# Moving a copy, a residual and a factor among ScalarE's and VectorE's work in a hybrid attention and pooling layer

## The chip, the core and the metric

The kernel runs on one core of a Trainium2 chip. The time is that of the device in microseconds (us) for one execution; the kernel before has a median of 1194.55 us over 3 runs (1194.26 to 1194.8). Lower is better. Two kernels computing the same output are compared: nothing in the arithmetic differs between them.

## The reference

One encoder layer over 4096 tokens of width 1024, in float32:

```
h    = RMSNorm(x) * pre_norm_g
q, k, v, g_a, u_p, g_p = split(h @ w_in)                  # w_in is 1024 x 2304
a    = banded_attention(q, k, v, bias, sink) * silu(g_a)  # 8 query heads, 2 kv heads, |i-j| <= 128
p    = pooling(u_p) * silu(g_p)                           # windows 2/4/8/16, a linear map per group
mix  = concat(a, p) @ w_out                               # 1024 x 1024
out  = x + RMSNorm(mix) * post_norm_g
```

In the attention each block of 128 queries sees three blocks of keys; a learned bias is added to the logits, and a learned sink takes part in the softmax.

## The kernel before

**Numbers and tiles.** A float32 operand is carried as two float16 tiles, a high part and the rest, so one product is three matmuls. `nc.tensor` is TensorE (PE in the profile), `nc.vector` VectorE (DVE), `nc.scalar` ScalarE (ACT), `nc.gpsimd` GpSimd (POOL), and `nc.sync` issues the DMAs (SP).

**Two stages.** The first, until about 480 us, normalises x, projects the gates and the pooling input, and writes parts of this to DRAM. The second goes backwards over 16 units of 256 tokens, from unit 15 to unit 0; a unit is two blocks of 128 queries, 2u and 2u+1. For a unit it projects k, v and q, forms the softmax of each block in two halves of four heads ("a visit"), and then multiplies the gated values with the output weights. The change touches only this last multiplication and what follows it.

**The output product.** It is a seven-product scheme over quarters of the matrices (`"11"`, `"22"`, `"12"`, `"s1"` to `"s4"`); the products are accumulated in three PSUM banks, `acc0` to `acc2`, and combined in float32 tiles `mo` on the way out. Product 11 goes into bank 0. `begin` (line 1568) lets ScalarE copy it to the upper half of `mo_0`, because it is wanted alone; product 12 is then accumulated on top of it in the same bank, so the first matmul of product 12 waits for the copy. When 12 is finished, two engines read bank 0: `square` (line 1573) on ScalarE sums squares for the norm, and `gain11` (line 1578) on VectorE multiplies by `post_norm_g` into the lower half of `mo_0`. The framework puts readers of one PSUM bank on different engines in the order in which the program names them, and makes the second wait for the first.

**The softmax of a visit.** Per head: `logits` on VectorE (line 1295) from PSUM, `exps` on ScalarE (1306), then once `denominators` on VectorE (1313 and the reciprocal 1316), then `probs` on ScalarE (1328, the scaled high part) and `rests` on VectorE (1336, the remainder), and last `turn` (1345), a transposing DMA from `pn` to `pt`, which `values` (1417, PE) reads.

**The end of a block.** `mean` computes the root on VectorE and GpSimd (1602, 1607), `residual` (1611) on VectorE forms `xr = mo * rs + xr` over 1024 columns, and `store` (1617) sends it out. `i = 0` is the unit's second block; its residual reads `mo_0`. There is one buffer for `mo_0` (`bufs=1`), so a unit's `begin` and the unit before it share that memory. GpSimd meanwhile runs `sum4` (1494), `low` (1456, the rest of a split) and a small copy of the sink's logit into the tiles `p` (1289), which the exponentials read.

**What sets the order.** Every call is put into a list with a due time, `due(t, fn, ...)`; `pe(us, ...)` advances the clock `now[0]` of the TensorE work by an estimate. The list is sorted by time and emitted in that order with manual scheduling: each engine executes its own instructions in exactly this order, and waits in that order. A due time matters only through the order of rows on an engine. The last units, 1 and 0, have a written table of their own, in which `gain11` already stands ahead of `square` and nothing is changed.

Of the kernel before, what the change touches and what calls it, by code (L numbers as in the profile page):

```python
# [19 lines left out]
D = 1024  # L20
# [19 lines left out]
O11, O12, O21, O22, OT1, OT2, OT4, OT3 = range(8)  # L40
# [94 lines left out]
def hybrid_layer(ctx: ExitStack, tc, io, out):  # L135
# [74 lines left out]
    with ExitStack() as actx:  # L210
# [689 lines left out]
        for j in range(4):  # L900
            ld(9.5 + 0.1 * j, wut[:, j], io["w_uT"][j], 0.5, w=[f"wut{j}"])
            z = turn("sq")
            for half in range(2):
                t = U0 + 4 * j + 2 * half
# [338 lines left out]
    def due(t, fn, *args):  # L1243
        plan.append((t, len(plan), fn, args))
# [261 lines left out]
    LO, HI = slice(0, 512), slice(512, D)  # L1506
# [123 lines left out]
    def pe(us, fn, *args):  # L1630

        due(now[0], fn, *args)
        now[0] += us
        return now[0]
# [27 lines left out]
    M = 2.6  # L1662

    def mix_p1(u):
        due(pe(M, product, u, "11", O11, 0) - 0.2, begin, u)

    def mix_p4(u):
        pe(M, product, u, "22", OT4, 2)

    def mix_p2(u):  # L1670
        t = pe(M, product, u, "12", O21, 0, True)
        due(t, square, u, 0, 0, 0)
        due(t + 0.1, gain11, u)

    def mix_p6(u):
        due(pe(M, product, u, "s2", OT2, 1), add, u, (0, HI), (0, HI), 1)
# [8 lines left out]
    def mix_p5(u):  # L1685
        t = pe(M, product, u, "s1", OT1, 1)
        due(t, add, u, (1, HI), (1, HI), 1)
        due(t + 0.7, square, u, 1, 1)
        due(t + 1.4, gain, u, 1, HI)
        finish(u, 1, t + 4.0)  # L1690

    def mix_p3(u):
        t = pe(M, product, u, "s4", O22, 1, True)
        due(t, add, u, (0, HI), (0, HI), 1)
        due(t + 0.7, square, u, 0, 1)
        due(t + 1.4, gain, u, 0, HI)
        finish(u, 0, t + 4.0, 6.4)

    def finish(u, i, t, late=0.0):

        due(t, mean, u, i)
        due(t + 2.0 + late, residual, u, i, slice(0, D))
        due(t + 3.4 + late, store, u, i, slice(0, D))

    u = NU - 1
# [10 lines left out]
    for b in reversed(range(2, NB)):  # L1718
        u = b // 2
# [13 lines left out]
        elif b == NB - 3:  # L1733
            due(free[1], load_wo, OT3)
            mix_p4(u + 1)
            mix_p1(u + 1)
            attend(b + 1)
            visit(b, 1)
            due(free[1], load_wo, OT1)
            due(free[1] + 8.0, load_wo, O22)  # L1740
            do_kv(u - 1, 1)
            mix_p2(u + 1)
            mix_p6(u + 1)
        elif b % 2:
            mix_p3(u + 2)
            do_kv(u - 1)
            attend(b + 1)
            visit(b, 1)
            mix_p4(u + 1)
            mix_p1(u + 1)  # L1750
            mix_p6(u + 1)
            mix_p2(u + 1)
        else:
            do_q(u - 1, 0, 2.0 * (b == NB - 2), int(b < NB - 4))
            if b < NB - 2:
                attend(b + 1)
            visit(b, 1)
            do_q(u - 1, 1, 2.0 * (b == NB - 2))
            due(now[0] + 2.1, load_x, u - 3)
            if b == NB - 2:  # L1760
                attend(b + 1)
            elif b > 2:
                mix_p7(u + 1)
                mix_p5(u + 1)
# [212 lines left out]
```

## Time and profile before

| what | value |
|---|---|
| median of 3 runs | 1194.55 us |
| the profiled execution | 1192.77 us |
| its span in the profile | 1190.9 us |
| granted TensorE clock | 0.999 |
| busy: PE, DVE, ACT, POOL | 1156.3, 939.4, 702.2, 302.5 us |
| second stage, 480 to 1190 us: PE, DVE, ACT | 691.8, 555.3, 435.7 us of 710 |

A timeline row gives start, duration, engine, line, operation, out<-in and count; in brackets stands the idle time before it and what ended it. Rows of one line that follow each other are merged: "x3" of 1.62 us is three instructions. Consecutive instructions of an engine overlap a little in the records. The profiled execution is a single one, 1.78 us below the median; its span leaves out 1.87 us of it.

### The profile page before, as it was taken

The numbers are of one execution on the slowest core, as the hardware profiler recorded it, in microseconds if no ns is written. First come the engines' busy times: TensorE is split into PE (matmuls) and PEld (weight loads), VectorE is DVE, ScalarE is ACT, GpSimd is POOL, SyncE is SP. The second block draws the span as 40 slices with busy tenths as digits, with TensorE's granted clock in tenths as the row PEclk, the third lists the DMA queues.
The fourth block names the chain that finished last, engine by engine and source line by source line (L and its number), as shares of the span: only waits on it lengthen the run. The fifth ranks groups of instructions, "written<-read, shape, count | busy, mean of one in ns | idle before, by whom it ended". The sixth has DMA issues, their size and how long they took to land. (4 is left out here: it accounts for less than half of the span.)

```text
span 1190.9 us, 31660 instructions
## 1 busy us (share of the span) xinstructions
PE 1156.3 (97%) x13176; PEld 887.1 (74%) x13176; DVE 939.4 (79%) x1834; ACT 702.2 (59%) x1459; POOL 302.5 (25%) x309
## 2 busy tenths in 40 slices
PE   5999999999999999899999999999999999999997
PEld 4998888888988888876667676676666767757643
DVE  6889996867888973567878877887887887788786
ACT  5865655545755541266566675666666666666672
POOL 0002111101101110202324433432532443343231
PEclk9999999999999999999999999999999999999999
DMA  8644587577657573387976875776876577587794
GB/s 313 213 122 153 167 274 249 171 239 257 222 169 248 160 208 118 115 253 198 234 180 135 202 194 121 197 194 162 173 187 173 139 203 180 137 189 159 157 248 124
DMA packets 292432, 224.51 MB, mean 189 GB/s; under 512 B 210704, under 2 KB 251920, under 8 KB 287680
## 3 DMA queue, kind: packets, MB, share of 16 engines
q1 hardware_dynamic: 292288, 222.48, 68.5%
q8 instruction: 103, 1.69, 0.6%
q14 instruction: 41, 0.34, 0.1%
HBM read 113.37 MB, written 60.33 MB: 146 GB/s over the span
## 5 line engine op out<-in xcount | busy, mean ns | idle before, releaser
L634 PEld LDWEIGHTS <-wq 128*128 128x128 f16 x4104 | 401.5, 98 | 52.7 <-issue 2.8
L634 PE MATMUL y<-xt,wq 128*128 128x256 f16 x1512 | 204.2, 273 | 0.9 <-ACT cc L742 0.9
L1336 DVE SCALAR_TENSOR_TENSOR pn<-p,rd,pn 128x384 f16<-128x384 f32 (+1 forms) x256 | 156.7, 654 | 30.5 <-ACT pn L1328 30.5
L1227 PE MATMUL aq<-xb,xb 128*128 128x256 f16 x1024 | 173.2, 273 | 0.0
L1306 ACT ACTIVATE p<-p,nm 128x385 f32<-128x385 f32 (+1 forms) x256 | 152.9, 599 | 33.3 <-DVE nm L1295 27.9
L1550 PE MATMUL ms<-wo,ys 128*128 128x512 f16 x720 | 162.9, 379 | 0.7 <-ACT pn L1328 0.6
L1295 DVE CUSTOM_DVE_ANT_0 p<-s,nt,nsink 128x384 f32<-128x384 f32 (+1 forms) x256 | 155.9, 666 | 1.3 <-PE s L1272 1.1
L1328 ACT ACTIVATE pn<-p,rd 128x384 f16<-128x384 f32 (+1 forms) x256 | 137.7, 598 | 30.1 <-issue 19.5
L1227 PEld LDWEIGHTS <-xb 128*128 128x128 f16 x1280 | 125.1, 98 | 22.8 <-issue 6.6
L1227 PE MATMUL aq<-xb,xt 128*128 128x256 f16 x512 | 139.6, 273 | 0.0
L1550 PEld LDWEIGHTS <-ys 128*128 128x128 f16 x720 | 69.0, 98 | 82.9 <-issue 3.0
L1550 PE MATMUL m<-wo,y 128*128 128x512 f16 x540 | 121.7, 379 | 6.0 <-ACT mo L1568 5.0
L304 POOL TENSOR_TENSOR yt<-yt,sg 128x512 f32<-128x512 f32 (+2 forms) x32 | 48.0, 1499 | 311.4 <-DVE yt L307 293.9
L1550 PEld LDWEIGHTS <-y 128*128 128x128 f16 x540 | 51.4, 98 | 71.7 <-issue 11.9
L1584 POOL TENSOR_TENSOR mo<-mo,gpost 128x512 f32<-128x512 f32 x39 | 63.8, 1635 | 96.3 <-ACT jkb L1573 95.1
L634 PE MATMUL plain<-xb,wq 128*128 128x256 f16 x576 | 68.8, 276 | 3.0 <-ACT xb L446 1.8
L1417 PE MATMUL o<-pt,vv 128*64 128x256 f16 x1128 | 68.0, 274 | 1.1 <-DMA pt<-pn 1.1
L634 PE MATMUL y<-xb,wq 128*128 128x256 f16 x504 | 68.8, 273 | 0.0
L634 PE MATMUL v<-xb,wq 128*128 128x256 f16 x504 | 68.6, 273 | 0.2 <-DVE cc L304 0.2
L1227 PEld LDWEIGHTS <-xt 128*128 128x128 f16 x640 | 62.6, 98 | 8.3
L634 PE MATMUL v<-xt,wq 128*128 128x256 f16 x504 | 68.6, 273 | 0.0
L634 PE MATMUL x<-xb,wq 128*128 128x256 f16 x504 | 68.3, 273 | 0.0
(207 smaller groups left out, 1852.8 us busy)
## 6 DMA issues: line engine op xcount, KB each, us to landing
nt<-in_xT SPq DMA_DIRECT2D x28, 512.0 KB, 5.3
x_scr<-xb SPq DMA_DIRECT2D x14, 1024.0 KB, 7.1
xb<-x_scr SPq DMA_DIRECT2D x14, 1024.0 KB, 7.5
xr<-in_x SPq DMA_DIRECT2D x28, 512.0 KB, 4.6
out<-xr SPq DMA_DIRECT2D x28, 512.0 KB, 2.6
xn<-in_x SPq DMA_DIRECT2D x27, 512.0 KB, 4.4
ga_scr<-cc SPq DMA_DIRECT2D x64, 128.0 KB, 2.1
raw<-in_w_out SPq DMA_DIRECT2D x16, 512.0 KB, 5.2
```

The source lines that it names most:

```text
L304: eng.tensor_tensor(out=out, in0=in0, in1=in1, op=op)
L634: nc.tensor.matmul(b[:, s], wq[:, slot[q, op], wv, s, k, :], x[:, xv, k, :], start=(first and k + s + wv + xv == 0), stop=(last and k == H ...
L1227: nc.tensor.matmul(acc, w[:, j, k, :], x[:, kh, v, kt, :], start=(n == 0), stop=(n == 3 * KT - 1),)
L1295: nc.vector.tensor_tensor_reduce(out=p_t[b, half][:, hh, :nk], in0=s_t[jj][:, gg, :nk], in1=bias[:, h, lo : lo + nk], scale=negc[:, h : h ...
L1306: nc.scalar.activation(p[:, hh, : nk + 1], p[:, hh, : nk + 1], AF.Exp, bias=nm_t[b, half][:, hh : hh + 1], scale=-1.0, accum_out=den_t[b, ...
L1328: nc.scalar.activation(prob_view(b, half)[:, 0, i], p_t[b, half][:, i, :nk], AF.Copy, scale=rd_t[b, half][:, i : i + 1],)
L1336: nc.vector.scalar_tensor_tensor(out=pn4[:, 1, i], in0=p_t[b, half][:, i, :nk], scalar=rd_t[b, half][:, i : i + 1], in1=pn4[:, 0, i], op0= ...
L1417: nc.tensor.matmul(o_ps[a, 2 * half : 2 * half + 2], v[:, vi, kt, a], pt[b, half][:, pi, g, :, i, :], start=(n == 0), stop=(n == last),)
L1550: nc.tensor.matmul(z_t[u, tag], y[:, k, yi, :], wo[o][:, wi, k, :], start=(n == 0 and acc is None), stop=(n == 3 * HK - 1), skip_group_che ...
L1584: eng.tensor_tensor(out=mo, in0=mo, in1=gpost[:, cs], op=ALU.mult)
```

## The change

Three edits in the functions that give due times:

- `mix_p1`: the copy of product 11 (`begin`) is due 0.8 us earlier.
- `mix_p2`: `gain11` is due first and `square` 0.1 us later; before, it was the other way round.
- `mix_p3`: the residual of the second block is issued as two halves of 512 columns, 0.7 us apart, where one of 1024 stood; `mean` and `store` keep their times. `finish` loses an argument that nobody uses any more.

```diff
     def mix_p1(u):
-        due(pe(M, product, u, "11", O11, 0) - 0.2, begin, u)
+        due(pe(M, product, u, "11", O11, 0) - 1.0, begin, u)
 ...
     def mix_p2(u):
         t = pe(M, product, u, "12", O21, 0, True)
-        due(t, square, u, 0, 0, 0)
-        due(t + 0.1, gain11, u)
+        due(t, gain11, u)
+        due(t + 0.1, square, u, 0, 0, 0)
 ...
         due(t + 1.4, gain, u, 0, HI)
-        finish(u, 0, t + 4.0, 6.4)
-
-    def finish(u, i, t, late=0.0):
+        due(t + 4.0, mean, u, 0)
+        due(t + 12.4, residual, u, 0, LO)
+        due(t + 13.1, residual, u, 0, HI)
+        due(t + 13.8, store, u, 0, slice(0, D))
+
+    def finish(u, i, t):
 
         due(t, mean, u, i)
-        due(t + 2.0 + late, residual, u, i, slice(0, D))
-        due(t + 3.4 + late, store, u, i, slice(0, D))
+        due(t + 2.0, residual, u, i, slice(0, D))
+        due(t + 3.4, store, u, i, slice(0, D))
```

ScalarE's rows around the copy in unit 9, before. `p_1` and `pn_1` are the exponentials and scaled probabilities of a visit, `m_9` is bank 0 with product 11 (and later 12), `jkb` the throwaway output of `square`, and the `ys` are operands of later products:

```order
L1306 ACTIVATE p_1_11431,den_1_11429<-p_1_11431,nm_1_11428 128x385 [waits DVE_49] x3
L1328 ACTIVATE pn_1_11460<-p_1_11431,rd_1_11430 128x384 [waits DMAHW4_49,DVE_49,Activation_49]
L1568 COPY mo_0_11463<-m_9_11443 128x512 [waits PE_49]
L1328 ACTIVATE pn_1_11460<-p_1_11431,rd_1_11430 128x384 [waits Activation_49]
L1328 ACTIVATE pn_1_11460<-p_1_11431,rd_1_11430 128x384
L1328 ACTIVATE pn_1_11460<-p_1_11431,rd_1_11430 128x384 [waits Activation_49]
L1452 CAST ys_9_11505<-at_11361 128x4x128
L1452 CAST ys_9_11507<-s_9_11411 128x4x128 [waits PE_49]
L1573 ACTIVATE jkb_00_11510,ss_11465<-m_9_11443 128x512
L1452 CAST ys_9_11610<-yf_9_10905 128x4x128 [waits Pool_49]
```

The same place in the changed kernel:

```order
L1306 ACTIVATE p_1_11436,den_1_11434<-p_1_11436,nm_1_11433 128x385 [waits DVE_49] x3
L1568 COPY mo_0_11463<-m_9_11448 128x512 [waits DVE_49,PE_49]
L1328 ACTIVATE pn_1_11470<-p_1_11436,rd_1_11435 128x384 [waits DMAHW4_49,Activation_49]
L1328 ACTIVATE pn_1_11470<-p_1_11436,rd_1_11435 128x384 [waits Activation_49]
L1328 ACTIVATE pn_1_11470<-p_1_11436,rd_1_11435 128x384
L1328 ACTIVATE pn_1_11470<-p_1_11436,rd_1_11435 128x384 [waits Activation_49]
L1452 CAST ys_9_11511<-at_11366 128x4x128
L1452 CAST ys_9_11513<-s_9_11416 128x4x128 [waits PE_49]
L1573 ACTIVATE jkb_00_11613,ss_11465<-m_9_11448 128x512 [waits DVE_49]
L1452 CAST ys_9_11616<-yf_9_10910 128x4x128 [waits Pool_49]
```

The copy moved past one scaled probability and now waits for VectorE as well as for PE; the first scaled probability lost its own wait on VectorE. The square now waits for VectorE.

VectorE's rows at the same place, before (`mo_0_10746` is the tile of unit 10, `mo_0_11463` that of unit 9, in the same memory):

```order
L1611 SCALAR_TENSOR_TENSOR xr_11017<-mo_0_10746,rs_0_11306,xr_11017 128x1024 [waits DMAHW3_49,DMAHW1_49,Pool_49]
L1313 TENSOR_SCALAR den_1_11429<-den_1_11429 128x4 [waits Activation_49]
L1316 RECIPROCAL rd_1_11430<-den_1_11429 128x4 [waits DVE_49]
L1336 SCALAR_TENSOR_TENSOR pn_1_11460<-p_1_11431,rd_1_11430,pn_1_11460 128x384 [waits DMAHW4_49,Activation_49]
L1336 SCALAR_TENSOR_TENSOR pn_1_11460<-p_1_11431,rd_1_11430,pn_1_11460 128x384 [waits Activation_49] x3
L1589 TENSOR_TENSOR mo_0_11463<-ms_9_11470,mo_0_11463 128x512 [waits PE_49]
L1578 TENSOR_TENSOR mo_0_11463<-m_9_11443,gpost 128x512 [waits Activation_49]
```

And in the changed kernel:

```order
L1611 SCALAR_TENSOR_TENSOR xr_11022<-mo_0_10745,rs_0_11311,xr_11022 128x512 [waits DMAHW3_49,DMAHW1_49,Pool_49]
L1313 TENSOR_SCALAR den_1_11434<-den_1_11434 128x4 [waits Activation_49]
L1316 RECIPROCAL rd_1_11435<-den_1_11434 128x4 [waits DVE_49]
L1611 SCALAR_TENSOR_TENSOR xr_11022<-mo_0_10745,rs_0_11311,xr_11022 128x512
L1336 SCALAR_TENSOR_TENSOR pn_1_11470<-p_1_11436,rd_1_11435,pn_1_11470 128x384 [waits DMAHW4_49,DVE_49,Activation_49]
L1336 SCALAR_TENSOR_TENSOR pn_1_11470<-p_1_11436,rd_1_11435,pn_1_11470 128x384 [waits Activation_49] x3
L1589 TENSOR_TENSOR mo_0_11463<-ms_9_11476,mo_0_11463 128x512 [waits DVE_49,PE_49]
L1578 TENSOR_TENSOR mo_0_11463<-m_9_11448,gpost 128x512 [waits PE_49]
```

The lower half of the residual stays where the whole one was, the upper half moved behind the reciprocal, and the factor (line 1578) waits for PE where it waited for ScalarE. The order of the rows on PE, GpSimd and SP is the same in both kernels. In unit 15 there is no residual yet and the copy keeps its place; there only the two readers of bank 0 change the direction of their wait.

## The prediction

> **What bounds the kernel now.** I read the busy shares first, then who waited for whom on TensorE (PE), then the timelines of the engines in unit 9, one of thirteen alike (units 14 to 2).
>
> The busy row of the page, and one row of PE's waits over the whole span (total us, times, longest):
>
> ```profile
> PE 1156.3 (97%) x13176; PEld 887.1 (74%) x13176; DVE 939.4 (79%) x1834; ACT 702.2 (59%) x1459; POOL 302.5 (25%) x309
> PE m L1550 <- ACT mo L1568: 5.0, 13, 0.5
> ```
>
> PE is busy for 97% of the span: only work taken from PE, or an idle gap of PE closed, can shorten the kernel. The second row is the gap that this change can reach: 13 waits of product 12 for ScalarE's copy of product 11, together 5.0 us. It is the ceiling of the gain. PE in unit 9, and one row from unit 12:
>
> ```profile
> 811.23 2.75 PE L1550 MATMUL m<-wo,y 128*128 128x512 f16 x12 [0.42 <-ACT mo L1568]
> 813.91 1.12 PE L1272 MATMUL s<-k_all,q 64*32 64x128 f16 x96
> 814.96 0.28 PE L1227 MATMUL aq<-xb,xb 128*128 128x256 f16 x1
> ...
> 820.31 2.16 PE L1417 MATMUL o<-pt,vv 128*64 128x256 f16 x36
> ...
> 823.45 0.28 PE L1227 MATMUL aq<-xb,xb 128*128 128x256 f16 x1
> ...
> 683.68 2.75 PE L1550 MATMUL m<-wo,y 128*128 128x512 f16 x12 [0.22 <-ACT mo L1568]
> ```
>
> Product 12 starts at 811.23 and PE was ready 0.42 earlier, at 810.81. Ten units wait 0.41 to 0.54; three (12, 8 and 4) wait 0.22 or 0.23, since PE comes 0.2 later there. No other row between these has a wait. ScalarE and VectorE at the same place:
>
> ```profile
> 808.53 0.18 ACT L1306 ACTIVATION_READ_ACCUMULATOR p<-p,nm 128x1 f32 x1
> 810.09 0.61 ACT L1328 ACTIVATE pn<-p,rd 128x384 f16<-128x384 f32 x1 [1.38 <-issue]
> 810.61 0.57 ACT L1568 COPY mo<-m 128x512 f32<-128x512 f32 x1
> 811.08 1.62 ACT L1328 ACTIVATE pn<-p,rd 128x384 f16<-128x384 f32 x3
> 812.61 0.60 ACT L1452 CAST ys<-at 128x512 f16<-128x512 f32 x1
> 814.02 0.62 ACT L1452 CAST ys<-s 128x512 f16<-128x512 f32 x1 [0.80 <-PE m L1550]
> 814.54 0.59 ACT L1573 ACTIVATE jkb<-m 128x512 bf16<-128x512 f32 x1
> 815.03 0.19 ACT L1573 ACTIVATION_READ_ACCUMULATOR jkb<-m 128x1 f32 x1
> 815.12 0.61 ACT L1452 CAST ys<-yf 128x512 f16<-128x512 f32 x1
> 817.16 0.62 ACT L1306 ACTIVATE p<-p,nm 128x385 f32<-128x385 f32 x1 [1.43 <-DVE nm L1295]
> ...
> 821.19 0.57 ACT L1216 ACTIVATE q<-aq 128x512 f16<-128x512 f32 x1
> ```
>
> ```profile
> 807.82 1.89 DVE L1611 SCALAR_TENSOR_TENSOR xr<-mo,rs,xr 128x1024 f32<-128x1024 f32 x1
> 809.64 0.16 DVE L1313 TENSOR_SCALAR den<-den 128x4 f32<-128x4 f32 x1
> 809.83 0.18 DVE L1316 RECIPROCAL rd<-den 128x4 f32<-128x4 f32 x1
> 810.74 0.62 DVE L1336 SCALAR_TENSOR_TENSOR pn<-p,rd,pn 128x384 f16<-128x384 f32 x1 [0.73 <-ACT pn L1328]
> 811.73 1.68 DVE L1336 SCALAR_TENSOR_TENSOR pn<-p,rd,pn 128x384 f16<-128x384 f32 x3 [0.37 <-ACT pn L1328]
> 813.32 0.69 DVE L1589 TENSOR_TENSOR mo<-ms,mo 128x512 f32<-128x512 f32 x1
> 815.26 0.69 DVE L1578 TENSOR_TENSOR mo<-m,gpost 128x512 f32<-128x512 f32 x1 [1.25 <-ACT jkb L1573]
> ...
> 821.80 0.69 DVE L1217 SCALAR_TENSOR_TENSOR q<-aq,q 128x512 f16<-128x512 f32 x1 [0.37 <-ACT q L1216]
> ```
>
> The exponentials end at 808.71 and ScalarE then stands idle until 810.09. The page calls this "issue", but the reciprocal's end at 810.01 gives the reason: the scaled probabilities need it, and it stands behind the 1.89 us residual. So the path to PE's gap is residual, denominator, reciprocal, one scaled probability, copy (810.61 to 811.18), product 12.
>
> **The residual in halves, and the copy in front.** These go together. The copy writes the memory that the residual of the unit before reads (one buffer), and in the new order it waits for VectorE, while the first scaled probability has lost its wait on VectorE. The copy's wait therefore covers the reciprocal and what stands behind it: the upper half of the residual. It does not start at 808.71. The new path is: lower half, denominator, reciprocal, upper half, copy, product 12. The prices of a half, from the groups of line 1611 (min/median/max in ns), and GpSimd beside it:
>
> ```profile
> L1611 DVE SCALAR_TENSOR_TENSOR xr<-mo,rs,xr x28: 1284/1591/2392, 582.9 to 1169.7; 128x1024 f32<-128x1024 f32 x28
> L1611 DVE SCALAR_TENSOR_TENSOR xb<-xb,rs,xb x4: 744/1018/1285, 1173.0 to 1183.6; 128x1024 f32<-128x1024 f32 x2, 128x512 f32<-128x512 f32 x2
> ```
>
> ```profile
> 807.37 1.27 POOL L1494 TENSOR_TENSOR yf<-yf,at 128x512 f32<-128x512 f32 x1
> ...
> 815.83 1.16 POOL L1456 TENSOR_TENSOR ys<-yf,ys 128x512 f16<-128x512 f32 x1
> 816.93 0.32 POOL L1289 COPY p<-nsink 128x4 f32<-128x4 f32 x2
> ```
>
> A whole residual at its shortest is 1.28, a half 0.744, say 0.75. The one in question took 1.89, 0.61 over its shortest, while GpSimd's line 1494 ran until 808.64. I charge the whole 0.61 to the lower half, which alone meets that instruction. Step by step: lower half 807.82 + 0.75 + 0.61 = 809.18. The next VectorE row starts 0.07 before the end (809.64 against 807.82 + 1.89), so the denominator starts at 809.11 and the reciprocal, 0.19 later, at 809.30. The upper half follows 0.13 after that (0.18 less some overlap), 809.43 to 810.18. ScalarE starts 0.08 after VectorE's end (810.09 against 810.01): copy 810.26 to 810.83. PE starts 0.05 after the copy (811.23 against 811.18): 810.88. The wait shrinks from 0.42 to 0.07.
>
> So ten units save 0.35, and three, where PE is ready 0.2 later, save their whole 0.22: 3.5 + 0.66 = **4.2 us**. Bounds: if the lower half meets no stall, the denominator is ready with the exponentials, 808.74, and all 5.0 us go. If the upper half is stalled by 0.61 too, it ends at 810.79, product 12 starts at 811.49, and each unit loses about 0.26. I take the value near the first, because no GpSimd row lies between 808.64 and the upper half's end.
>
> The Trainium skill has a rule for the stall: SBUF — State Buffer, section "Who interferes with whom", says that a VectorE instruction with two SBUF inputs and a GpSimd instruction that reads SBUF exclude each other, the loser waiting for the other's whole instruction. By it the whole residual would have ended at 808.64 + 1.28 = 809.92; the trace has 809.71, so the rule's sign agrees and its size is 0.21 too large here. It returns among the rivals.
>
> **What is late next on ScalarE and VectorE.** The copy and the four probabilities are the same work in another order: probabilities 810.73 to 812.86 (spacing 0.51), against an end of 812.70. The rests follow 0.05 behind: end 813.57 against 813.41, and the transposing DMA starts 0.16 later. Its row, and the time to landing:
>
> ```profile
> L1345 SPq DMA_TRANSPOSE pt<-pn x1: 3627/3627/3627, 813.5 to 813.5; - x1
> DMA to landing us min/median/max: 7.0/7.0/7.0
> ```
>
> It was issued at 813.47 and landed at 820.47. Line 1417 at 820.31 reads this half in its second 18 matmuls, from 821.39: 0.92 to spare. Later by 0.16 and wanted 0.35 earlier, it keeps 0.41. The store ahead of it on SP waits for the upper half, done at 810.2, and stays ahead. The addition (line 1589) moves from 813.32 to 813.49 and ends at 814.18; the projection that reuses its bank, at 814.96, now wants it at 814.61. Both cost nothing.
>
> **The factor in front of the square.** Before, the factor waited 1.25 us for the square, and the next logits stood behind it. Now it follows the addition, 814.10 to 814.79 (product 12 ends at 810.88 + 2.75 = 813.63, before it). The square waits for it: 814.83 instead of 814.54, and behind it on ScalarE the cast of `ys`, 815.41 instead of 815.12. GpSimd's `low` waits for this cast (ends 816.02): 816.09 instead of 815.83, then its copy into `p`, 817.19 instead of 816.93, and the exponentials need that copy: before, they started 0.07 after its first half, at 817.16. So earlier logits gain nothing; the exponentials come 0.26 later. Behind them on ScalarE stands the conversion of q (821.19, now 821.45) and VectorE's (821.80 to 822.49, now to 822.75), which frees the bank for the projection at 823.45, now 823.10. That leaves 0.35, less about 0.05 of signalling. Cost nothing, but the cover is thin: without it, each 0.1 us costs 13 × 0.1 = 1.3 us.
>
> In unit 15 the square, held by the factor behind the last rests, delays ScalarE's casts once; no product needs them for several microseconds. I take zero.
>
> **Sum.** The profiled execution, 1192.77 us with a span of 1190.9, becomes 1188.6 and 1186.7. The median lies 1.78 above it: 1194.55 − 4.2 = **1190.4 us**.
>
> **Rivals.**
>
> *A: the next wait eats part of it.* The conversion of q or the transposed tile comes late by more than its 0.3 or 0.4. For: both margins shrink by 0.5 to 0.6. Against: in the rows above each still holds. A slip of 0.2 beyond the margin gives back 2.6 us: 1193.0; of 0.35, all.
>
> *B: GpSimd holds the lower half until its own end.* Then the lower half ends at 808.64 + 0.75 = 809.39, 0.21 later than I said; product 12 starts at 811.09, and 13 × 0.14 = 1.8 us are saved: 1192.7. Against it stands the recorded end of the whole residual, 0.21 earlier than this gives. This is the time by that page's rule.
>
> *C, slower: the upper half runs slow.* The longest residual took 2.392, so a half can meet a stall of 0.6 and more. The copy, with all four probabilities behind it, is then later than before: +0.26 in each unit, 13 × 0.26 = 3.4 us, 1197.9. It decides from a stall of 0.35, where the upper half ends at 810.53 and the copy starts at 810.61, as before. Against: no GpSimd work is near.
>
> *D: the copy waits only for the exponentials and PE.* All of 5.0 us is saved: 1189.6. It is the ceiling; the lost wait of the first probability speaks against it.
>
> **How the numbers follow.** About 0.2%, 2.4 us, is what a measurement of this kernel tells from no change. Forecast (a gain of 3 to 5) 0.64; A 0.16; B 0.08; C 0.08; D 0.04. Faster by over 0.2% are the forecast, D and a third of A: 0.74. Within 0.2%: B and the rest of A, and a little of C: 0.19. Slower: 0.07. The likeliest case's own range is 1189.3 to 1191.7. The range that holds 8 in 10 takes in D, B and most of A, and leaves C out: 1189.0 to 1193.4.
>
> **What would show it.** In the changed profile: PE's wait for line 1568 at 1 us or less in all instead of 5.0; two residual rows of 512 per unit, the first about 1.36, the second about 0.75, and the copy 0.08 after the second; the factor with no wait for `jkb`, the square about 0.3 later against the addition. Wrong it would be if the second half shows over 1.1 us, or if PE shows a new wait before line 1227 (on q) or line 1417 (on `pt`) in most units.

## The result, and the profile after

The changed kernel takes **1190.57 us** (median of 6 runs, 1188.44 to 1190.99) beside 1194.67 us for the kernel before (6 runs, 1194.26 to 1196.88). The ratio is 0.996, with a 95% interval of 0.9947 to 0.9973: about 4 us faster. The forecast was 1190.4.

The profiled execution took 1190.99 us, with a span of 1189.2. Its busy row, and the longest of PE's waits over the whole span (total us, times, longest):

```profile
PE 1159.2 (97%) x13176; PEld 889.0 (75%) x13176; DVE 938.2 (79%) x1847; ACT 703.5 (59%) x1459; POOL 302.4 (25%) x309
```

```profile
PE sp L370 <- DMA ident<-in_ident: 7.0, 1, 7.0
PE n2ga L528 <- ACT sq L519: 3.9, 1, 3.9
PE s L1272 <- ACT q L1216: 3.8, 2, 3.1
```

The row "PE m L1550 <- ACT mo L1568" is gone, and no new row stands in its place: the waits listed come once or twice each, and the kernel before had the like of the large ones. Two small new waits do not show in this list; they are read from starts below. Thirteen more VectorE instructions (1847 for 1834) are the halves of the residual.

**A span can hide part of a gain.** The span fell by only 1.7 (1190.9 to 1189.2), the median by 4.1. The difference lies ahead of the loop. Three rows of the table of stretches (stretch, its length, busy us of PE, PEld, DVE, ACT and POOL, granted clock, DMA share, GB/s), of before and of after:

```profile
500.00:510.00 10.00, 6.56 (x100) 5.33 (x98) 3.49 (x11) 4.77 (x13) 0.00 (x0) 1.00 0.93 343
```

```profile
500.00:510.00 10.00, 6.57 (x86) 4.62 (x85) 3.49 (x11) 4.54 (x12) 0.00 (x0) 0.76 0.94 348
510.00:520.00 10.00, 8.89 (x112) 7.05 (x111) 4.67 (x15) 4.65 (x15) 0.19 (x1) 0.90 0.89 341
```

In this execution the granted clock fell to 0.76, and PE did 86 matmuls in the stretch in place of 100. The copy of unit 15, the first of the loop, starts at 545.15 for 542.69. A better measure of the loop is the time from unit 14's copy to unit 2's, twelve units later, from the rows of line 1568 in that stretch (min/median/max in ns, then the first and last start), of before and of after:

```profile
L1568 ACT COPY mo<-m x13: 566/567/567, 597.4 to 1109.5; 128x512 f32<-128x512 f32 x13
```

```profile
L1568 ACT COPY mo<-m x13: 586/586/587, 599.4 to 1107.9; 128x512 f32<-128x512 f32 x13
```

To two decimals the loop took 512.15 before and 508.45 after: 3.70 in twelve units. Most units went from 42.52 to 42.20 us. This number is used for all kernels below, because it leaves the start of the program out.

**Unit 9 after.** The timelines of PE, ScalarE and VectorE, as the prediction showed them for before:

```profile
809.13 2.75 PE L1550 MATMUL ms<-wo,ys 128*128 128x512 f16 x12
811.91 2.75 PE L1550 MATMUL m<-wo,y 128*128 128x512 f16 x12
814.59 1.12 PE L1272 MATMUL s<-k_all,q 64*32 64x128 f16 x96
```

```profile
811.27 0.59 ACT L1568 COPY mo<-m 128x512 f32<-128x512 f32 x1 [1.49 <-DVE xr L1611]
811.76 2.13 ACT L1328 ACTIVATE pn<-p,rd 128x384 f16<-128x384 f32 x4
...
815.85 0.60 ACT L1573 ACTIVATE jkb<-m 128x512 bf16<-128x512 f32 x1 [0.53 <-DVE mo L1578]
...
818.45 0.62 ACT L1306 ACTIVATE p<-p,nm 128x385 f32<-128x385 f32 x1 [1.40 <-POOL p L1289]
```

```profile
808.89 1.36 DVE L1611 SCALAR_TENSOR_TENSOR xr<-mo,rs,xr 128x512 f32<-128x512 f32 x1
810.18 0.16 DVE L1313 TENSOR_SCALAR den<-den 128x4 f32<-128x4 f32 x1
810.37 0.18 DVE L1316 RECIPROCAL rd<-den 128x4 f32<-128x4 f32 x1
810.47 0.72 DVE L1611 SCALAR_TENSOR_TENSOR xr<-mo,rs,xr 128x512 f32<-128x512 f32 x1
...
814.53 0.69 DVE L1589 TENSOR_TENSOR mo<-ms,mo 128x512 f32<-128x512 f32 x1
815.13 0.68 DVE L1578 TENSOR_TENSOR mo<-m,gpost 128x512 f32<-128x512 f32 x1
```

The new path is there step by step: lower half 808.89 to 810.25, denominator, reciprocal, upper half 810.47 to 811.19, copy at 811.27 (waiting for `xr`, 0.08 after it) to 811.86, product 12 at 811.91, 0.05 after that. The factor at 815.13 no longer waits for `jkb`; the square waits 0.53 for the factor.

**Starts, not idle columns.** Product 12's row carries no idle bracket any more, yet it does still wait. A row of twelve such matmuls is 2.75 long, but the next row begins before its end: 811.91 + 2.75 = 814.66, and the scores start at 814.59. What counts is the distance between starts. Unit 7, PE before and after:

```profile
893.75 2.75 PE L1550 MATMUL ms<-wo,ys 128*128 128x512 f16 x12
896.91 2.75 PE L1550 MATMUL m<-wo,y 128*128 128x512 f16 x12 [0.41 <-ACT mo L1568]
...
907.88 0.93 PE L1272 MATMUL s<-k_all,q 64*32 64x288 f16 x48
908.74 0.28 PE L1227 MATMUL aq<-xb,xb 128*128 128x256 f16 x1
```

```profile
894.10 2.75 PE L1550 MATMUL ms<-wo,ys 128*128 128x512 f16 x12
896.88 2.75 PE L1550 MATMUL m<-wo,y 128*128 128x512 f16 x12
...
907.85 0.93 PE L1272 MATMUL s<-k_all,q 64*32 64x288 f16 x48
908.80 0.27 PE L1227 MATMUL aq<-xb,xb 128*128 128x256 f16 x1
```

From product s2 (`ms`) to product 12 (`m`) it is 3.16 before and 2.78 after. In the experiments below it is 2.59 where the copy is early enough. So the true wait was about 0.58 per unit before, where the bracket says 0.41, and 0.19 is still there after. In units 12, 8 and 4 it was 2.98 before and is 2.59 after: there the whole wait of 0.39 is gone. All thirteen units therefore gained about 0.39.

**Two new losses.** The last two rows of each fence above show the first. From the second scores to the next projection of q it is 0.86 before and 0.95 after. What it waits for is VectorE's conversion of q, which frees its bank; after, unit 7:

```profile
908.06 0.69 DVE L1217 SCALAR_TENSOR_TENSOR q<-aq,q 128x512 f16<-128x512 f32 x1 [0.36 <-ACT q L1216]
```

It ends at 908.75, and the projection starts at 908.80; PE would have been ready at 907.85 + 0.86 = 908.71. Eight units lose such 0.09, and units 13, 9 and 5 nothing.

Units 11 and 10 lose 0.20 each at another place. Unit 11, the values' row on PE before and after, and the transposing DMA that feeds its second half, after:

```profile
735.08 2.15 PE L1417 MATMUL o<-pt,vv 128*64 128x256 f16 x36
```

```profile
736.13 2.35 PE L1417 MATMUL o<-pt,vv 128*64 128x256 f16 x36
```

```profile
L1345 SPq DMA_TRANSPOSE pt<-pn x1: 3627/3627/3627, 730.0 to 730.0; - x1
DMA to landing us min/median/max: 7.2/7.2/7.2
```

The row is 0.20 longer. Its first 18 matmuls run as before; the 19th starts at 737.31, 10.06 after product 12, where unit 7 has 9.89, and the transposed tile lands at 737.27. The scores behind it come 0.20 later, so the conversion of q is in time there.

Over the loop this adds up to 12 × 0.39 − 7 × 0.09 − 2 × 0.20 = 3.65 us, measured 3.70. For all thirteen units it is 13 × 0.39 − 8 × 0.09 − 2 × 0.20 = 3.95, beside the 4.1 between the medians.

### The profile page after: what moved, and what is told of

It reads as the page before. It is cut to its first block, busy times and chain, and to the rows that moved or that the text cites. A ratio compares the mean times of both kernels' runs of the same rounds, so it can differ in the third digit from the quotient of the medians.

```text
span 1189.2 us, 31697 instructions
## 1 busy us (share of the span) xinstructions
PE 1159.2 (97%) x13176; PEld 889.0 (75%) x13176; DVE 938.2 (79%) x1847; ACT 703.5 (59%) x1459; POOL 302.4 (25%) x309
## 4 chain that ended last, share of the span: by engine, by line
PE 51%; DVE 1%; DMA 1%; ACT 0%; issue 0%; DVEq 0%; POOLq 0%; ACTq 0%
PE aq L1227 13%; PE ms L1550 12%; PE m L1550 9%; PE o L1417 5%; PE s L1272 4%; PE kv L1373 3%; PE kv L1227 3%; PE z L1522 1%; DMA pt<-pn 1%; PE s L1522 0%; DVE p L1295 0%; DVE pn L1336 0%; DVE xr L1611 0%; ACT pn L1328 0%; DVE s L1485 0%
## 5 line engine op out<-in xcount | busy, mean ns | idle before, releaser
L1550 PE MATMUL ms<-wo,ys 128*128 128x512 f16 x720 | 162.8, 379 | 0.6 <-ACT pn L1328 0.6
L1550 PEld LDWEIGHTS <-ys 128*128 128x128 f16 x720 | 69.0, 98 | 82.7 <-issue 2.6
L1550 PE MATMUL m<-wo,y 128*128 128x512 f16 x540 | 121.7, 379 | 1.5 <-POOL y L1456 0.7
L1550 PEld LDWEIGHTS <-y 128*128 128x128 f16 x540 | 51.3, 98 | 66.7 <-issue 6.5
L1272 PE MATMUL s<-k_all,q 64*32 64x288 f16 (+7 forms) x3648 | 63.5, 268 | 5.0 <-ACT q L1216 3.8
```

The source lines that it names most:

```text
L1272: nc.tensor.matmul(s_ps[qs, gg, c0:c1], q_t[u, half][a, qi, jj, tl + 32 * hq : tl + 32 * hq + 32], k_all[a, ki, kc + c0 - s0 : kc + c1 - s ...
L1550: nc.tensor.matmul(z_t[u, tag], y[:, k, yi, :], wo[o][:, wi, k, :], start=(n == 0 and acc is None), stop=(n == 3 * HK - 1), skip_group_che ...
```

## The experiments

Two questions were open: which of the three edits does the work, and which of the two readings of PE's wait is right, the 5.0 us of the idle column or the about 7.0 us of the starts (10 × 0.58 + 3 × 0.39). The first four and the kernel before ran on one chip (before: 1193.82, 15 runs), the last four and the kernel before on another (1194.31, 15 runs). Diffs of the first four are against the kernel before, those of the last three against the changed kernel.

**Only the copy moved.**

```diff
     def mix_p1(u):
-        due(pe(M, product, u, "11", O11, 0) - 0.2, begin, u)
+        due(pe(M, product, u, "11", O11, 0) - 1.0, begin, u)
```

> The kernel before with one edit: the copy of product 11 in front of the first scaled probability; the residual stays whole and ahead of the denominator, the square stays ahead of the factor. Theory of the prediction (the copy waits for the residual of the unit before, which shares its memory, and for nothing later): the copy starts 0.08 us after the whole residual, in unit 9's terms 809.71 + 0.08 = 809.79, 0.8 us earlier than before; product 12 no longer waits, so all 5.0 us go: about 1189.6 us, PE's wait for line 1568 gone. The first scaled probability moves from 810.09 to about 810.27. Rival (the copy in front needs the halved residual to gain anything): the wait of 0.42 us stays or a new wait takes its place, 1193.5 to 1195.

Measured: 1186.14 us, ratio 0.9937 (0.9925 to 0.995), a gain of 7.7; the loop took 505.96, that is 6.2 less in twelve units. Unit 7, PE, VectorE and ScalarE:

```profile
889.59 2.75 PE L1550 MATMUL ms<-wo,ys 128*128 128x512 f16 x12
892.18 2.75 PE L1550 MATMUL m<-wo,y 128*128 128x512 f16 x12
```

```profile
889.36 1.90 DVE L1611 SCALAR_TENSOR_TENSOR xr<-mo,rs,xr 128x1024 f32<-128x1024 f32 x1
891.18 0.16 DVE L1313 TENSOR_SCALAR den<-den 128x4 f32<-128x4 f32 x1
```

```profile
891.34 0.59 ACT L1568 COPY mo<-m 128x512 f32<-128x512 f32 x1 [1.09 <-DVE den L1313]
```

The whole residual ends at 891.26 and the copy starts 0.08 later, at 891.34. (The view names the denominator, which also ended at 891.34; 0.08 after the residual is the distance that the changed kernel has too.) Ahead of the copy stand one residual of 1.90 and nothing else, where in the changed kernel stand two halves with the denominator and the reciprocal between them: 808.89 to 811.19, 2.30. The copy ends at 891.93, and PE comes to product 12 at 892.18, so that the copy has 0.2 to spare. This edit alone gets all of the wait at product 12. The ratio's interval stands for a gain of 6.0 to 9.0 us; it holds the 7.0 of the starts and not the 5.0 that the prediction called the ceiling. Against the wait won stands a loss of 0.07 to 0.09 in units 13, 9 and 5, where the first projection of q behind product 12 starts later than before; what holds it was not followed. Over the loop, 9 × 0.58 + 3 × 0.39 − 3 × 0.08 = 6.15 us, measured 6.2.

**Only the halves.**

```diff
-        finish(u, 0, t + 4.0, 6.4)
+        due(t + 4.0, mean, u, 0)
+        due(t + 12.4, residual, u, 0, LO)
+        due(t + 13.1, residual, u, 0, HI)
+        due(t + 13.8, store, u, 0, slice(0, D))
```

> The kernel before with one edit: the residual in two halves around denominator and reciprocal; the copy stays behind the first scaled probability. Theory: the denominator comes 0.5 us earlier, the first scaled probability starts at about 809.56 in unit 9's terms, and the copy then waits for the upper half, which ends at 810.18: it starts at about 810.26, as in the changed kernel, and product 12 waits 0.07 us or less. Gain 4.2 us, 1190.4. Rival (the order of the copy on ScalarE is what gains): the wait of 0.42 us stays, 1194.6.

Measured: 1188.58 us, ratio 0.9957 (0.9944 to 0.9971), a gain of 5.2; loop 507.48. VectorE and ScalarE in unit 7:

```profile
891.28 1.36 DVE L1611 SCALAR_TENSOR_TENSOR xr<-mo,rs,xr 128x512 f32<-128x512 f32 x1
...
892.85 0.72 DVE L1611 SCALAR_TENSOR_TENSOR xr<-mo,rs,xr 128x512 f32<-128x512 f32 x1
```

```profile
893.01 0.62 ACT L1328 ACTIVATE pn<-p,rd 128x384 f16<-128x384 f32 x1 [0.84 <-ACT p L1306]
893.65 0.59 ACT L1568 COPY mo<-m 128x512 f32<-128x512 f32 x1
```

The reciprocal comes earlier because only a half stands ahead of it, the first scaled probability runs beside the upper half, and the copy starts at 893.65, 0.08 after that half ends. The spacing from s2 to product 12 is 2.78, as in the changed kernel, and the projection of q does not wait (0.86 in all units). Thirteen times 0.39 is 5.1; measured 5.2. With the halves in place, the move of the copy gains nothing at product 12: whichever of the two stands first, the copy waits for the upper half.

**Only the factor in front of the square.**

```diff
         t = pe(M, product, u, "12", O21, 0, True)
-        due(t, square, u, 0, 0, 0)
-        due(t + 0.1, gain11, u)
+        due(t, gain11, u)
+        due(t + 0.1, square, u, 0, 0, 0)
```

> The kernel before with one edit: the factor ahead of the square. Theory: PE's waits of 0.42 us for the copy stay, 5.0 us in all; the square starts about 0.25 us later, the exponentials behind it 0.25 us later, and no PE wait appears: within 0.5 us of 1194.6. Rival (the factor's 1.25 us wait for the square is what limits): logits 1.2 us earlier shorten the unit, 1191 or less. Other rival (the later exponentials reach PE): new waits of line 1227, 1195.5 or more.

Measured: 1194.18 us, ratio 1.0002 (0.9993 to 1.001, 11 runs); loop 512.15, as before. PE's wait for the copy is unchanged:

```profile
PE m L1550 <- ACT mo L1568: 5.0, 13, 0.5
```

By itself this edit changes nothing that the times show: as long as PE is late for product 12, the later exponentials still have room.

**GpSimd's line 1494 earlier.** This tests the price of 0.61 that the prediction put down to GpSimd. In the kernel before, `sum4` stands behind a split (line 1456) on GpSimd and meets the residual; here it goes ahead of the split. Nothing else changes.

```diff
     def sums(u, t):
 ...
-        due(t + 5.0, sum4, u)
+        due(t + 0.6, sum4, u)
```

> The kernel before with GpSimd's subtraction of line 1494 put ahead of the split of ys (line 1456) on GpSimd, so that it ends before the residual begins; none of the three edits. Theory (the residual's 0.61 us over its shortest time comes from GpSimd running beside it): the residual of line 1611 falls from 1.89 to 1.28 to 1.45, the denominator and the copy come 0.45 to 0.55 us earlier, PE's wait for line 1568 goes: 1189.6 to 1190.2. Rival (it comes from elsewhere, ScalarE or a DMA): the residual stays at 1.89 and the wait at 0.42, 1194.6.

Measured: 1189.48 us, ratio 0.9957 (0.9945 to 0.997), a gain of 4.3; loop 505.81. All residuals of that form, GpSimd and VectorE in unit 7:

```profile
L1611 DVE SCALAR_TENSOR_TENSOR xr<-mo,rs,xr x28: 1283/1296/2389, 584.5 to 1164.3; 128x1024 f32<-128x1024 f32 x28
```

```profile
889.22 1.27 POOL L1494 TENSOR_TENSOR yf<-yf,at 128x512 f32<-128x512 f32 x1 [1.55 <-DVE at L1491]
890.46 1.16 POOL L1456 TENSOR_TENSOR ys<-at,ys 128x512 f16<-128x512 f32 x1
```

```profile
891.39 1.31 DVE L1611 SCALAR_TENSOR_TENSOR xr<-mo,rs,xr 128x1024 f32<-128x1024 f32 x1
```

The median residual fell from 1591 to 1296 ns, and the one in question from 1.90 to 1.31, so line 1494 beside it was the cause of the 0.6. With that gone, product 12 starts 2.59 after s2, with the copy where it always was. The loop gains as much as with the copy moved (6.3). The median gains less. In the profiled execution the span is 4.9 shorter, not 6.3: 0.7 are lost ahead of the first copy, 0.25 up to the second, and 0.5 behind unit 2's copy. Ahead of the first copy the granted clock was lower, 0.84 for 1.00 at 500 to 510 us. Between the first two, one single wait of PE grew from 0.6 to 1.5:

```profile
PE ms L1550 <- ACT pn L1328: 1.5, 1, 1.5
```

Where the last 0.5 come from stays open.

**The changed kernel once more**, unchanged, beside the next three on their chip.

> The changed kernel once more, on the chip of the next three. Theory now: PE's start-to-start spacing from product s2 to product 12 is 2.78 us (3.17 before, 2.59 with no wait), and the second projection of q waits 0.08 us for the conversion of q in the units whose scores are not cut in two; a unit takes 42.20 us, 3.7 to 4.2 us below the kernel before.

Measured: 1189.73 us, ratio 0.9961 (0.9949 to 0.9974); loop 508.42. As at first, with the transposed tile late in units 11 and 10 again, and by 0.09 in unit 12.

**The changed kernel without the swap**, that is copy and halves.

```diff
-        due(t, gain11, u)
-        due(t + 0.1, square, u, 0, 0, 0)
+        due(t, square, u, 0, 0, 0)
+        due(t + 0.1, gain11, u)
```

> The changed kernel without the third edit: the copy in front and the residual in halves, but the square ahead of the factor as before. Theory (the factor in front delays the square, the cast behind it, GpSimd's split and small copy, the exponentials and so the conversion of q): spacing s2 to 12 stays 2.78, the 0.08 us ahead of the second projection goes, a unit takes 42.13 us as with the halves alone, about 0.9 us less in all than the changed kernel. Rival (the 0.08 us come from the halves or the copy): they stay, 42.20.

Measured: 1190.45 us, ratio 0.9964 (0.9952 to 0.9977); loop 508.17. The times do not tell it from the changed kernel. The 0.9 us that were expected do not show. The timelines do tell them apart: the projection of q starts 0.86 after the second scores in every unit (1.05 in units 13, 9 and 5), and the undisturbed units take 42.13 us for 42.20. So the swap is the cause of the 0.09, which is worth less than 1 us in all.

Units 12, 11 and 10 took 0.16 to 0.24 more, which hides that in the sum. It is the late transposed tile again, so the swap is not its cause. In these units the second half of the values starts 10.03 to 10.11 after product 12, for 9.89. Copy and halves together issue the transfer 2.77 after product 12; it was 2.24 before, 2.25 with the halves alone and 2.4 to 2.6 with the copy alone. In units 11 and 10 it lands 7.2 to 7.3 later, at 9.99 and 10.05 (unit 12's transfer is not in the records). With one of the two edits alone, no unit waits more than 0.03 for it.

**The changed kernel without the halves**, that is copy and swap.

```diff
-        due(t + 4.0, mean, u, 0)
-        due(t + 12.4, residual, u, 0, LO)
-        due(t + 13.1, residual, u, 0, HI)
-        due(t + 13.8, store, u, 0, slice(0, D))
+        finish(u, 0, t + 4.0, 6.4)
```

(`finish` has its argument `late` back; it gives the whole residual at t + 12.4, and `mean` and `store` the times that they had.)

> The changed kernel without the halves: the copy in front, the whole residual ahead of the denominator, the factor ahead of the square. Theory (the upper half behind the reciprocal is what holds the copy in the changed kernel): the copy waits for the whole residual only, spacing s2 to 12 falls to 2.59; the factor follows the addition 0.19 us earlier than in the changed kernel, so the conversion of q ends about 0.1 us before PE wants the bank, no wait there: a unit takes 41.93 to 41.95 us, 3 to 4 us less in all than the changed kernel, within 1 us of the copy in front alone. Rival (the factor's place costs the same wherever the copy stands): a wait of 0.1 us or more ahead of the second projection, 42.05 or more.

Measured: 1187.43 us, ratio 0.9942 (0.9928 to 0.9955); loop 505.91. The spacing is 2.59, the second projection of q does not wait, and no transposed tile is late; the first projection starts 0.06 to 0.09 later in units 13, 9 and 5, as with the copy alone. Without the halves the changed kernel gains 2.3 us more, where 3 to 4 were expected. The swap costs nothing here (the loop is 505.96 with the copy alone). VectorE and PE in unit 7:

```profile
897.84 0.68 DVE L1578 TENSOR_TENSOR mo<-m,gpost 128x512 f32<-128x512 f32 x1
...
905.79 0.69 DVE L1217 SCALAR_TENSOR_TENSOR q<-aq,q 128x512 f16<-128x512 f32 x1 [0.37 <-ACT q L1216]
```

```profile
894.83 2.75 PE L1550 MATMUL m<-wo,y 128*128 128x512 f16 x12
...
906.67 0.28 PE L1227 MATMUL aq<-xb,xb 128*128 128x256 f16 x1
```

The factor starts 3.01 after product 12, where it was 3.22 in the changed kernel's unit 9 (815.13 against 811.91), and the conversion of q ends at 906.48, 0.19 ahead of the projection. In this order of the rest, the swap fits.

**Half a microsecond of work behind the square.** This measures how near the conversion of q is to PE's path. An extra copy of 512 columns, whose result nobody reads, is put behind the square on ScalarE, ahead of the cast of `ys`; it takes 0.61 us.

```diff
+    extra = pb1.tile([P, 512], F32, name="extra")
+
+    def more(n):
+        nc.scalar.copy(extra[:, :n], gpost[:, :n])
 ...
         due(t + 0.1, square, u, 0, 0, 0)
+        due(t + 0.11, more, 512)
```

> The changed kernel with one more instruction on ScalarE right behind the square, a copy of 128x512 from one constant tile to a tile that nobody reads (0.48 us from start to start), in units 15 to 2. It delays the cast behind it. Theory (the chain cast, GpSimd's split, its small copy, exponentials, conversion of q ends at PE with nothing to spare): the second projection waits 0.56 us in place of 0.08 in ten units and about 0.2 us in three: 5 to 5.5 us more than the changed kernel. Rival (the 0.08 us are not on this chain, ScalarE has room): less than 1 us more.

Measured: 1195.56 us, ratio 1.001 (1.0001 to 1.0019, 10 runs), 5.8 more than the changed kernel on that chip; loop 513.38. PE's wait, and unit 7's PE:

```profile
PE aq L1227 <- DVE q L1217: 4.5, 10, 0.5
```

```profile
908.10 0.93 PE L1272 MATMUL s<-k_all,q 64*32 64x288 f16 x48
909.57 0.27 PE L1227 MATMUL aq<-xb,xb 128*128 128x256 f16 x1 [0.53 <-DVE q L1217]
```

From the scores to the projection it is now 1.47, so PE waits 0.61, about 0.52 more than in the changed kernel (0.95). The cast behind the added copy starts 0.51 later after product 12 (902.16 − 897.13 = 5.03, for 4.52 in the changed kernel), and all of it lands on PE. Unit times give 0.51 for the eight units that already waited for q, about 0.38 for units 11 and 10, which had waited for the tile, and about 0.2 for units 13, 9 and 5: 8 × 0.51 + 2 × 0.38 + 3 × 0.2 = 5.4, beside the 5.8 between the medians. In the eight there is no slack left on that chain in the changed kernel.

## Why the prediction was right

**The total was right, with some luck: its terms were off in opposite directions.** Predicted were 10 × 0.35 + 3 × 0.22 = 4.2 us. The trace shows 13 × 0.39 − 8 × 0.09 − 2 × 0.20 = 3.95 us. The path to the copy was right; about 0.9 more was gained on it than was summed, and 1.1 was lost where two margins were read as enough.

- *The path to the copy: right.* Lower half 1.36 (predicted 1.36), upper half 0.72 (0.75), copy 0.08 behind it, PE 0.05 behind the copy. From product s2 to product 12 the prediction implies 3.17 − 0.35 = 2.82; measured 2.78.
- *The stall by GpSimd falls on the lower half alone: right.* The upper half never met it, and moving line 1494 away took 0.6 off the residual. The Trainium skill's rule (SBUF — State Buffer, section "Who interferes with whom") had the loser wait for the other's whole instruction, which was the prediction's rival B. By it the lower half would have taken about 1.57; it took 1.36. The rule names the right pair of engines and is 0.2 too large here. Rival C, a slow upper half, did not occur either: all thirteen took 0.72.
- *"It is the ceiling of the gain", 5.0 us: wrong.* This is the first mis-sized term. The idle column measures from the modelled end of a row to the next start, and rows of twelve such matmuls end 0.16 too late by that model (2.75 long, 2.59 from start to start): the wait was 0.58 per unit, and 0.39 in units 12, 8 and 4, together 7.0. The prediction's own rows held the hint: product 12 from 811.23 with 2.75 ends at 813.98, and the next row starts at 813.91. So the three units gained 0.39 and not 0.22, and rival D's time of 1189.6 was no floor: moving the copy alone gives 1186.14.
- *"Cost nothing, but the cover is thin", for the factor: wrong by 0.09 in eight units.* This is the second one. The margin of 0.35 was read in unit 9, and unit 9 is one of three (13, 9 and 5) that have more than the rest. There the two runs of scores behind product 12 are 96 matmuls of 1.05, elsewhere 48 of 0.86: 2 × 0.19 = 0.38 more time for the conversion of q. With 0.35 − 0.38 the margin in the other ten is −0.03, and with 0.05 of signalling that is the loss measured. The shift itself was right: the exponentials start 6.54 after product 12 in unit 9, where it was 5.93 before; predicted was 0.26 + 0.35 = 0.61 more. In units 11 and 10 it does not show, because the tile of the next point is later still. What the prediction named as a sign that it was wrong, a new wait ahead of line 1227 in most units, is there.
- *"It keeps 0.41", for the transposed tile: wrong in units 11 and 10.* This is the third. The shift was right: issued 0.54 later after product 12 (2.24 to 2.78; predicted 0.16 + 0.35 = 0.51). The margin was again read in unit 9 alone, where the second half of the values is wanted 10.08 after product 12 and not 9.89, and with that unit's landing of 7.0. From unit to unit the landing took 5.5 to 7.3. In units 11 and 10 it is at the long end, so the tile lands 10.02 after product 12. Both halves of rival A thus began, with 1.1 us given back where it had put 2.6.
- *"These go together", the copy and the halves: a step that was not priced apart.* The copy needs the memory that the whole residual reads. Halves with the reciprocal between them make the reciprocal earlier, which helps the copy where it stands behind a scaled probability, and make the residual's end later (2.30 for 1.90 after its start), which hurts a copy that waits for nothing else. Each of the two edits closes the gap by itself, the halves by two thirds and the copy fully. Together they close it by two thirds too, and bring the late tile: the loop gains 6.2 with the copy, 4.7 with the halves and 4.0 with both.

The span of the profiled execution was predicted as 1186.7 and was 1189.2. The loop accounts for 3.7 of the gain; the rest of the difference is the stretch at 500 to 520 us, where the clock was lower.

## What to carry to other kernels

Measure a stall as the difference of starts against the same work without a stall, and not by the idle column alone: here the column showed 5.0 us of 7.0. Read a margin in every kind of unit and not in one, since three of thirteen had 0.38 more slack for q and 0.19 more for the tile than the rest; where a DMA is in the path, read its longest landing. Price each edit of a group by itself along the chain that it shortens, because two edits that attack one wait do not add up, and the smaller one can take from the larger: moving one copy gave 1186 us, and all three edits together 1190.

## What the runs showed of the hardware

An instruction of GpSimd can cost one of VectorE time where they overlap. Line 1494 with 0.82 of it beside the residual cost VectorE 0.6; line 1494 itself took 1.27 there and 1.27 in its earlier place, so GpSimd lost nothing. With line 1494 moved, line 1456 (1.16) runs 0.23 into the residual, which took 1.31, 0.03 over its shortest. Why the one costs most of the shared time and the other little was not settled.

Transposing DMAs of one line, all from `pn` to `pt` behind product 12, took 5.5 to 7.3 us from issue to landing within one execution of the changed kernel.

Runs of one kernel differ by about 3 us, with the mean granted clock: moving the copy alone took 1185.31 us at 0.999 and 1188.36 at 0.996. A gain of 1 us, like that of taking the swap out, can be seen in the spacing of rows in a trace, and not in the medians of five runs.
